# Early weight splits in two batches at wider spacing, operand sets loaded closer together, x stored a step later

## The chip, the core and the metric

The kernel runs on one core of a Trainium2 chip. The core has a matrix engine (TensorE, PE in the profile, with its weight loads as PEld), a vector engine (VectorE, DVE), a scalar engine (ScalarE, ACT), GpSimd (POOL) and a queue engine that here only issues transfers (SyncE, SP). The metric is device time in microseconds of the whole program. Before the change the median of 3 runs is 2904.11 us (2894.93 to 2907.33).

## The reference, cut to what matters

One layer of a decoder step in float32 for 1024 prompt tokens and 64 sample tokens (8 sequences of 8), model width 1024:

```python
x = x + 0.5 * swiglu(rmsnorm(x, norm_ffn1), ffn1_w_in, ffn1_w_out)      # first FFN
mix = token_mixing(rmsnorm(x, norm_mix), ...)                           # projection, pooling and SSD branches
x = x + mix
x = x + 0.5 * swiglu(rmsnorm(x, norm_ffn2), ffn2_w_in, ffn2_w_out)      # second FFN
y = rmsnorm(x, norm_final)

def swiglu(x, w_in, w_out):          # w_in 1024 x 5632, w_out 2816 x 1024
    gu = x @ w_in
    return (silu(gu[..., :2816]) * gu[..., 2816:]) @ w_out
```

`token_mixing` multiplies by `w_in` (1024 x 8224), runs a causal pooling branch (`pool_w_group`, `pool_w_out`) and a chunked SSD scan (`ssd_w_out`), gates them and multiplies by `w_o`. The new pooling, convolution and SSD states are outputs too.

## The kernel before, in words

**Number format.** Each float32 operand of a large product is cut into a high part that TensorE takes at full rate and the remainder: `hi = round(x)` on ScalarE, `lo = x - hi` on VectorE. A product is then three matmuls: weight-high by hi, weight-high by lo, weight-low by hi. Weights come from HBM as 128 x 512 pieces of 256 KB (`wraw`) and are cut into `wh` and `wl`.

**Stages in time.** First FFN: three plain column blocks, then pairs by a seven-product (Strassen-like) scheme, `pw`, which needs seven sums of weights, cut one after the other; its results go through GpSimd into seven operand sets in HBM (`hc...`). The output product (`po`) runs through these seven sets one by one (list `OUTER`, index p): each set is 11 tiles `hr`, loaded back and cut into `hh` and `hr`, while the set before is multiplied; the sums land in x tiles. Projection stage: the same seven-product scheme over `w_in` pairs (`pw` again), with convolution, pooling window sums and gates behind each pair. Then the mixing stage (scan, `pso`, `pwo`), and the second FFN, with the same code as the first.

**Early splits.** The weights that are used more than once later (four column blocks of `w_in`, the pooling group weights, `pool_w_out`, `ssd_w_out`, `w_o` and the plain blocks of the second FFN) are cut ahead of time by `part_weights`: 88 jobs, in the order of the list `early`. In step i the generator issues the load of job i (`wr`, L354), then the two stores of job i-2 (high part L361, low part L362, 256 KB each, to a DRAM tile `wp`), then the split of job i-1 (ScalarE L403, VectorE L405, both in `split`). Later stages load the ready parts (L342). Each job takes two tiles of the stage's shared ring `fx` (16 tiles, tag `fx`), which also holds the results of the pairs, x tiles and temporaries.

**What sets the order.** The program is written as generators ("chains"). `pe[0]` is a planner's clock that counts matmul time in us; a chain yields how long it wants to wait, and `tick()` after each matmul group steps the chains that are due. `later(d, fn)` is a chain of one step. A scheduler then orders the instructions of each engine, gives tiles their buffers, and puts waits where a buffer has to come free. All large transfers go through SP's queue in order: a transfer that waits for its source or for a buffer holds those behind it. The number of transfers under way is bounded as well: the issue of one waits for the end of one some eight issues earlier.

**The numbers that the change touches.** `W_AT, W_NEXT = 108.0, 3.7` start the early splits at planner time 108 and space their steps. `H_AT[1]`, `H_PACE[1]` (3.0 and 2.5) say when, after the start of set p, the loads of set p+1 begin, and their spacing; index 0 is for the first set. In the output product of the first FFN finished x tiles are written to HBM (`xspill`, L819) right after they are merged (L786) and squared for the next norm. The second FFN uses `H_AT` and `H_PACE` as well, but stores no x there.

Of the kernel before, what the change touches and what calls it, by code (L numbers as in the profile page):

```python
# [75 lines left out]
N_PRE = 3  # L76
Y_PACE = 0.8
G_WAIT, G_LAST, GP_LAST = (6.0, 12.0), (2.5, 3.0), (2.5, 1.2)
H_AT, H_PACE, H_LAND, H_CUT = (1.0, 3.0), (0.9, 2.5), 4.5, 0.9
N_SUM = 1  # L80
B_AT, B_PACE, HN_WAIT = 3.0, 7.0, 22.0
W_AT, W_NEXT = 108.0, 3.7
AHEAD = 4
ACC_AT, RD_WAIT, Y_LOAD = 4.0, 6.0, 0.6

# [2 lines left out]
def tile_hybrid_pool_ssd_macaron(  # L88
# [11 lines left out]
    dma = nc.sync.dma_start  # L100
# [7 lines left out]
    def nm(s):  # L108
        uid[0] += 1
        return f"{s}_{uid[0]}"  # L110
# [20 lines left out]
    def fx(dt=F32, name="x"):  # L131
        if stage["name"] == "mix":
            return act((P, 576), dt, name)
        return stage["p"].tile([P, FXW], dt, tag="fx", bufs=N_FX, name=nm(name))

    def psum(tag="ps", name="ps"):
        npd = stage["npd"]
        return stage["ps"].tile([P, 512], F32, tag=tag, bufs=npd if tag == "pd" else 8 - npd, name=nm(name))
# [4 lines left out]
    pe = [0.0]  # L143
# [13 lines left out]
    def start(gen, delay=0.0):  # L157
        c = Chain(gen, delay)
        chains.append(c)
        return c  # L160

    def later(delay, fn):
        def g():
            fn()
            return
            yield

        return start(g(), delay)
# [9 lines left out]
    def tick():  # L178
        while chains:
            c = min(chains, key=lambda q: q.due)  # L180
            if c.due > pe[0]:
                return
            c.step()
# [5 lines left out]
    def mm(out, lhsT, rhs, start=True, stop=True, free=False):  # L189
        pin(T.matmul(out, lhsT, rhs, start=start, stop=stop, skip_group_check=free))  # L190
        pe[0] += max(out.free_size(), 64) / 2400.0 * (1 if rhs.dtype == F32R else 4)
# [90 lines left out]
    xspill = [[dp.tile([P, NTOK[h]], F32, tag=f"xs{h}_{m}", name=f"xspill{h}_{m}") for m in range(KD)] for h in HALVES]  # L282
# [60 lines left out]
            out.append(t.bitcast(F32R).rearrange("p (k c) -> p k c", c=ncol))  # L343
        return out

    def part_weights(jobs):


        held, t0 = {}, pe[0]
        for i in range(len(jobs) + 2):  # L350
            if i < len(jobs):
                w, k0, nk, c0, ncol = jobs[i]
                t = fx(name="wr")[:, : nk * ncol]
                dma(t.rearrange("p (k c) -> p k c", c=ncol),  # L354
                    w[k0 * P : (k0 + nk) * P, c0 : c0 + ncol].rearrange("(k p) c -> p k c", p=P))
                held[i] = t, fx(F32R, name="wp")[:, : nk * ncol]
            if i >= 2:
                w, k0, nk, c0, ncol = jobs[i - 2]
                t, a = held.pop(i - 2)
                d = dp.tile([P, 2, 4 * P], F32, tag=f"wp{len(parted)}", name=nm("wp"))  # L360
                dma(d[:, 0, : nk * ncol], a.bitcast(F32))  # L361
                dma(d[:, 1, : nk * ncol], t)  # L362
                parted[id(w), k0, c0] = d
            if 1 <= i <= len(jobs):
                t, a = held[i - 1]
                split(t, a, t.bitcast(F32R))
            yield max(0.1, t0 + W_NEXT * (i + 1) - pe[0])

    def products(out, Wh, Wl, kk, cs, xs, k, nk):
        for ps_, (W, lo_) in enumerate(((Wh, False), (Wh, True), (Wl, False))):  # L370
# [30 lines left out]
    def split(src, hi, lo, scale=1.0):  # L401

        S.activation(hi, src, AF.Identity, scale=scale)  # L403
        if isinstance(scale, float) and scale == 1.0:
            V.tensor_tensor(lo, src, hi.bitcast(F32), op=ALU.subtract)  # L405
        else:
            V.scalar_tensor_tensor(lo, src, scale, hi.bitcast(F32), op0=ALU.mult, op1=ALU.subtract)
# [297 lines left out]
    def ffn(wi, wo, prep, after, half=None, sums=None):  # L705
# [17 lines left out]
        def feed(p):  # L723


            hi, lo = parts[p] = [], []
            todo, last, k = [], 0.0, 0
            while k < N_K2 or todo:
                if k < N_K2:
                    t, a = act(name="hr")[:, :HALF_T], act((P, 576), F32R, "hh")[:, :HALF_T]  # L730
                    dma(t, hc[OUTER[p][0]][k])
                    todo.append((pe[0], t, a))
                    k += 1
                    yield H_PACE[p > 0]
                while todo and todo[0][0] + H_LAND < pe[0] and last + H_CUT < pe[0] or k == N_K2 and todo:
                    if k == N_K2:
                        yield max(0.2, todo[0][0] + H_LAND - pe[0], last + H_CUT - pe[0])
                    _, t, a = todo.pop(0)
                    split(t, a, t.bitcast(F32R))
                    hi.append(a)  # L740
                    lo.append(t.bitcast(F32R))
                    last = pe[0]

        def out_raw(blocks, m, kb, nk):

            raws = [raw_w(wo, ki * N_K2 + kb, nk, (mi * 4 + m) * P) for mi, ki, _ in blocks]
            if len(raws) == 1:
                return raws[0]
            t = stage["p"].tile([P, 4 * P], F32, tag="wsum", bufs=N_S, name=nm("ws"))[:, : nk * P]
            with tc.high_priority(hp[0]):  # L750
                G.tensor_tensor(t, *raws, op=ALU.add if blocks[1][2] > 0 else ALU.subtract)  # L751
            return t

        def out_weights(t, nk):

            wh, wl = (sp.tile([P, 4 * P], F32R, tag=n_, bufs=N_W, name=nm(n_))[:, : nk * P] for n_ in ("wh", "wl"))
            with tc.high_priority(hp[0]):
                S.activation(wh, t, AF.Copy)
                V.tensor_tensor(wl, t, wh.bitcast(F32), op=ALU.subtract)  # L759
            return [w.rearrange("p (k c) -> p k c", c=P) for w in (wh, wl)]  # L760
# [14 lines left out]
        def x_tile(h, m):  # L775
            if xs[h][m] is None:
                xs[h][m] = t = fx(name="x")[:, : NTOK[h]]
                dma(t, xspill[h][m])
# [9 lines left out]
        for p, (_, blocks, dests) in enumerate(OUTER):  # L788
            if p + 1 < len(OUTER):
                feeds[p + 1] = start(feed(p + 1), H_AT[1])  # L790
            for m in range(4):
                for mi in sorted({d[0] for d in dests}):
                    for h in HALVES:
                        x_tile(h, mi * 4 + m)
                pts = [psum("pd", "po") for _ in range(2)]
                for kb in range(0, N_K2, 4):
                    n4 = min(4, N_K2 - kb)
                    while len(summed) <= min(at + N_SUM, len(chunks) - 1):
                        summed.append(out_raw(*chunks[len(summed)]))
                    wh, wl = out_weights(summed[at], n4)  # L800
                    summed[at] = None
                    at += 1
                    for kk in range(n4):
                        k = kb + kk
                        while len(parts[p][0]) <= k:
                            feeds[p].step()
                        hi, lo = parts[p][0][k], parts[p][1][k]
                        for i, (W_, X_) in enumerate(((wh, hi), (wh, lo), (wl, hi))):
                            for j, pt in enumerate(pts):
                                mm(pt[:, :HT], W_[:, kk, :], X_[:, j * HT : (j + 1) * HT],  # L810
                                   start=k == 0 and i == 0, stop=k == N_K2 - 1 and i == 2)
                        tick()
                for mi, ti, sign in dests:
                    merge(pts, mi, m, ti, sign)
                if p in ENDS and sums:
                    h, q = ENDS[p]
                    x = xs[h][q * 4 + m]
                    squares(sums[h], x)
                    dma(xspill[h][q * 4 + m], x)  # L819
            if p in ENDS:  # L820
                h, q = ENDS[p]
                if half and p in (1, 5):
                    half(h, q, xs[h])
                if p in (4, 6):
                    after(h, xs[h])
# [119 lines left out]
    early = [(W, kb, 4, c0, P) for c0 in [OFF_Z + j * P for j in range(N_ZP)] for kb in (0, 4)]  # L945
# [57 lines left out]

    start(turn(), TURN_AT)
    start(load_consts(), CONST_AT)
    start(part_weights(early), W_AT)
    hp[0] = HP
    ffn(wi1, ffn1_w_out[0], prep1, after1, sums=sums1)

# [193 lines left out]
    def pool_in():  # L1203
        src = state_pool[0].rearrange("b r d -> (b r) d")
        sin = []
        for q in range(2):
            t = fx(name="spin")[:120]
            dma(t[:, :512], src[:, q * 512 : (q + 1) * 512])
            sin.append(t)
        return sin, [fx(name="ost")[:79] for _ in range(2)]  # L1210
# [118 lines left out]
        ends.clear()  # L1329

    zs = list(range(N_ZP, 16, 2))
    sin, ost = pool_in()
    for k in range(0, KD, 2):
        u_pair(k, sin, ost)
# [644 lines left out]
```

## Time and profile before

| what | value |
|---|---|
| runs, median (range) | 2904.11 us (2894.93 to 2907.33) |
| profiled execution, its own time | 2903.95 us |
| its span, first to last instruction | 2902.1 us |
| mean granted TensorE clock | 0.988 |
| PE busy | 2789.8 us, 96% |
| DVE, ACT, POOL busy | 1802.6, 1339.0, 1189.0 us (62%, 46%, 41%) |
| moved by DMA | 595.61 MB, mean 205 GB/s |
| `pw` of the first FFN, first to last matmul | 110.8 to 562.9 us |
| `po` of the first FFN | 563.1 to 818.2 us |
| `pw` of the projection stage | 874.6 to 1524.8 us |
| `pw` and `po` of the second FFN | 2231.1 to 2638.8 and 2638.9 to 2885.3 us |
| early splits, first to last (ACT) | 146.9 to 544.3 us |

In a table of stretches each row has the stretch in us, its length, then for each engine the busy time and in brackets the number of instructions, the granted clock as a share of full speed, the busy share of the DMA engines, and GB/s. A list of waits has "engine, line waited for <- what ended the wait: us in total, times, longest".

### The profile page before, as it was taken

What the parts mean: (1) busy time and instruction counts of PE and PEld (TensorE: products, weight loads), DVE (VectorE), ACT (ScalarE), POOL (GpSimd) and SP (SyncE); (2) the same over time, 40 slices, a digit from 0 to 9 for tenths busy, and PEclk for the clock granted to TensorE, in tenths of its full rate; (3) what the DMA queues carried; (4) which work ended last, traced back from release to release, by engine and by line L of the source; (5) the groups of instructions that cost most, each with busy time, mean ns of one, the idle gap of its engine ahead of it and who ended that gap; (6) DMA issues with size and microseconds to landing.
All of it is one profiled execution on the core that took longest, in us unless ns stands there. A gap on an engine that the chain in (4) does not pass through costs nothing. (4 is left out here: it accounts for less than half of the span.)

```text
span 2902.1 us, 56345 instructions
## 1 busy us (share of the span) xinstructions
PE 2789.8 (96%) x20898; PEld 2660.8 (92%) x20898; DVE 1802.6 (62%) x2949; ACT 1339.0 (46%) x2830; POOL 1189.0 (41%) x1152
## 2 busy tenths in 40 slices
PE   7999999899999999999999989999999999999998
PEld 6998999899989999999997777778999999999997
DVE  6555566766765787566745775765346544448764
ACT  5344444533443456555556765554123333335433
POOL 5444546624243333343421333543115654554422
PEclk9999999999999999999999999999999999999999
DMA  5588899898763333233349879988875422339864
GB/s 138 158 273 268 293 296 290 282 278 263 244 209 111 112 102 119 91 101 110 107 139 314 277 283 307 326 289 251 278 256 184 150 94 94 98 98 298 266 204 158
DMA packets 614725, 595.61 MB, mean 205 GB/s; under 512 B 56922, under 2 KB 430800, under 8 KB 614442
## 3 DMA queue, kind: packets, MB, share of 16 engines
q1 hardware_dynamic: 613078, 589.62, 63.3%
q8 instruction: 164, 2.69, 0.4%
q10 hardware_dynamic: 1372, 2.40, 0.2%
q14 instruction: 111, 0.91, 0.1%
HBM read 419.52 MB, written 172.58 MB: 204 GB/s over the span
## 5 line engine op out<-in xcount | busy, mean ns | idle before, releaser
L190 PE MATMUL pw<-hi,wh 128*128 128x288 f32 (+1 forms) x2176 | 634.4, 292 | 16.1 <-ACT t L604 8.3
L190 PE MATMUL pw<-X,wh 128*128 128x256 f32 (+1 forms) x3264 | 626.2, 290 | 10.5 <-ACT t L602 5.8
L190 PE MATMUL pw<-hi,wl 128*128 128x288 f32 (+1 forms) x2176 | 631.0, 290 | 5.4 <-DVE wl L502 5.4
L190 PE MATMUL pw<-lo,wh 128*128 128x288 f32 (+1 forms) x2176 | 629.6, 289 | 0.0
L190 PEld LDWEIGHTS pw<-X,wh 128*128 128x128 f32 x3264 | 516.5, 190 | 13.8 <-ACT t L602 7.9
L190 PE MATMUL pw<-X,wl 128*128 128x256 f32 (+1 forms) x1632 | 471.2, 289 | 0.8 <-DVE wl L502 0.8
L190 PEld LDWEIGHTS pw<-hi,wh 128*128 128x128 f32 x2176 | 414.2, 190 | 21.0 <-ACT t L604 9.8
L190 PEld LDWEIGHTS pw<-hi,wl 128*128 128x128 f32 x2176 | 413.9, 190 | 7.3 <-DVE wl L502 7.2
L190 PEld LDWEIGHTS pw<-lo,wh 128*128 128x128 f32 x2176 | 414.3, 190 | 0.0
L502 DVE TENSOR_TENSOR wl<-s,wh 128x512 fp32r<-128x512 f32 x284 | 255.9, 903 | 200.9 <-ACT wh L501 195.6
L495 POOL TENSOR_TENSOR s<-wraw,wraw 128x512 f32<-128x512 f32 x142 | 202.8, 1428 | 359.8 <-DVE wl L502 165.4
L190 PEld LDWEIGHTS pw<-X,wl 128*128 128x128 f32 x1632 | 311.0, 191 | 1.1 <-DVE wl L502 1.0
L501 ACT ACTIVATE wh<-s 128x512 fp32r<-128x512 f32 x284 | 179.0, 630 | 234.5 <-PE pw L190 172.2
L751 POOL TENSOR_TENSOR ws<-wraw,wraw 128x512 f32<-128x512 f32 (+1 forms) x120 | 165.4, 1381 | 275.2 <-DMA wraw<-in_ffn_w_out_dram 155.9
L190 PE MATMUL po<-hh,wh 128*128 128x272 f32 x1232 | 259.6, 292 | 9.2 <-ACT hh L403 6.6
L190 PE MATMUL po<-hh,wl 128*128 128x272 f32 x1232 | 258.8, 291 | 4.2 <-DVE wl L759 4.0
L190 PE MATMUL po<-hr,wh 128*128 128x272 f32 x1232 | 257.7, 290 | 1.6 <-DVE hr L405 1.6
L502 DVE TENSOR_TENSOR wl<-wraw,wh 128x512 fp32r<-128x512 f32 x213 | 176.7, 830 | 80.0 <-ACT wh L501 74.0
L190 PEld LDWEIGHTS po<-hh,wh 128*128 128x128 f32 x1232 | 196.8, 190 | 11.3 <-ACT hh L403 7.1
L501 ACT ACTIVATE wh<-wraw 128x512 fp32r<-128x512 f32 x213 | 133.7, 629 | 155.2 <-PE pw L190 137.7
L190 PEld LDWEIGHTS po<-hh,wl 128*128 128x128 f32 x1232 | 196.9, 190 | 6.1 <-DVE wl L759 5.9
L190 PEld LDWEIGHTS po<-hr,wh 128*128 128x128 f32 x1232 | 196.8, 189 | 2.3 <-DVE hr L405 2.3
(397 smaller groups left out, 5538.7 us busy)
## 6 DMA issues: line engine op xcount, KB each, us to landing
wraw<-in_ffn_w_out_dram SPq DMA_DIRECT2D x192, 256.0 KB
wraw<-in_ffn_w_in_dram SPq DMA_DIRECT2D x184, 256.0 KB
wraw<-wp SPq DMA_DIRECT2D x176, 256.0 KB
wraw<-in_w_in_dram SPq DMA_DIRECT2D x124, 256.0 KB
wp<-wp SPq DMA_DIRECT2D x88, 256.0 KB
wp<-wr SPq DMA_DIRECT2D x88, 256.0 KB
wh<-wp SPq DMA_DIRECT2D x88, 256.0 KB
wl<-wp SPq DMA_DIRECT2D x88, 256.0 KB
```

The source lines that it names most:

```text
L190: pin(T.matmul(out, lhsT, rhs, start=start, stop=stop, skip_group_check=free))
L495: G.tensor_tensor(t, a, b, op=op)
L501: S.activation(wh, a, AF.Copy)
L502: V.tensor_tensor(wl, a, wh.bitcast(F32), op=ALU.subtract)
L751: G.tensor_tensor(t, *raws, op=ALU.add if blocks[1][2] > 0 else ALU.subtract)
```

## The change

Three edits. `part_weights` takes its spacing as an argument, and the 88 jobs are started in two batches: the first 36 in the first FFN at planner time 108 with spacing 8.0, the other 52 in the projection stage, from planner time 20 after the start of its pairs, with spacing 9.0. The loads of the operand sets after the first begin at 2.0 instead of 3.0 and are 2.2 instead of 2.5 apart, in both FFNs. The store of a finished x tile in the first FFN is put 2.0 planner us later.

```diff
-H_AT, H_PACE, H_LAND, H_CUT = (1.0, 3.0), (0.9, 2.5), 4.5, 0.9
+H_AT, H_PACE, H_LAND, H_CUT = (1.0, 2.0), (0.9, 2.2), 4.5, 0.9
...
-W_AT, W_NEXT = 108.0, 3.7
+W_AT, W_NEXT, N_EARLY = 108.0, (8.0, 9.0), 36
...
-    def part_weights(jobs):
+    def part_weights(jobs, pace):
...
-            yield max(0.1, t0 + W_NEXT * (i + 1) - pe[0])
+            yield max(0.1, t0 + pace * (i + 1) - pe[0])
...
-                    dma(xspill[h][q * 4 + m], x)
+                    later(2.0, lambda h=h, i=q * 4 + m, x=x: dma(xspill[h][i], x))
...
-    start(part_weights(early), W_AT)
+    start(part_weights(early[:N_EARLY], W_NEXT[0]), W_AT)
...
     zs = list(range(N_ZP, 16, 2))
+    start(part_weights(early[N_EARLY:], W_NEXT[1]), 20.0)
```

How the order of instructions moves is shown at three places. The first is SP's queue in the first FFN, at the store of the mixture `hcs_2_269` (operand set s3, tile 2). Before:

```order
L354 DMA wr_2347<-in_pool_w_group_dram 128x2x256
L361 DMA wp_2350<-wp_2237 128x512
L362 DMA wp_2350<-wr_2235 128x512
L361 DMA wp_2405<-wp_2292 128x512
L362 DMA wp_2405<-wr_2290 128x512
L659 DMA hcb_2_258<-g_2085 128x544
L354 DMA wr_2402<-in_pool_w_group_dram 128x2x256
L361 DMA wp_2486<-wp_2349 128x512
L362 DMA wp_2486<-wr_2347 128x512
L521 DMA wraw_2683<-in_ffn_w_in_dram 128x4x128
L666 DMA hcs_2_269<-s_408_2429 128x544
```

And now:

```order
L354 DMA wr_2343<-in_w_in_dram 128x4x128
L361 DMA wp_2479<-wp_2235 128x512
L362 DMA wp_2479<-wr_2233 128x512
L644 DMA hcs_2_280<-g_2069 128x32
L666 DMA hcs_2_269<-s_393_2389 128x544
L643 DMA hcd_2_247<-g_2023 128x512
L907 DMA xin_400_2456<-in_x_prompt_dram 128x512
L354 DMA wr_2476<-in_w_in_dram 128x4x128
L354 DMA wr_2587<-in_w_in_dram 128x4x128
L361 DMA wp_2590<-wp_2345 128x512
L362 DMA wp_2590<-wr_2343 128x512
```

Ahead of this store there stood two loads and six stores of early splits in eleven rows (eight of eleven); now one load and two stores stand ahead of it, and at that point the jobs are at the blocks of `w_in` and no longer at the pooling weights.

The second is ScalarE's queue in the projection stage, at the start of a pair (`rb` takes the first product `pw`; `ct` is the convolution of the pair before). Before:

```order
L1026 COPY rb_14650<-pw_2499_14636 128x256
L1088 ACTIVATE ct_14653<-ra_14385,cols 128x512
L1088 ACTIVATE ct_14653<-crs_14620,cols 128x64
L501 ACTIVATE wh_14768<-s_2512_14725 128x512
L1026 COPY rb_14672<-pw_2503_14658 128x288
L1097 ACTIVATE ct_14653<-ct_14653 128x576
```

And now:

```order
L1026 COPY rb_14418<-pw_2413_14404 128x256
L1088 ACTIVATE ct_14421<-ra_14137,cols 128x512
L1088 ACTIVATE ct_14421<-crs_14388,cols 128x64
L501 ACTIVATE wh_14544<-s_2429_14501 128x512
L1026 COPY rb_14440<-pw_2417_14426 128x288
L403 ACTIVATE wp_14316<-wr_14314 128x512
L501 ACTIVATE wh_14586<-s_2438_14584 128x512
L1097 ACTIVATE ct_14421<-ct_14421 128x576
```

An early split (L403) now stands between the copy of a product and the next weight split (L501); behind it the queue goes on as before.

The third is SP's queue in the output product of the first FFN, from tile 9 of the operand set b22 (`hcb_9_265`) on. Before:

```order
L731 DMA hr_8201<-hcb_9_265 128x544
L305 DMA wraw_8364<-in_ffn_w_out_dram 128x4x128
L305 DMA wraw_8401<-in_ffn_w_out_dram 128x3x128
L305 DMA wraw_8403<-in_ffn_w_out_dram 128x3x128
L305 DMA wraw_8440<-in_ffn_w_out_dram 128x4x128
L305 DMA wraw_8442<-in_ffn_w_out_dram 128x4x128
L305 DMA wraw_8480<-in_ffn_w_out_dram 128x4x128
L305 DMA wraw_8482<-in_ffn_w_out_dram 128x4x128
L305 DMA wraw_8519<-in_ffn_w_out_dram 128x3x128
L819 DMA xspill_7_91<-x_7671 128x512
L731 DMA hr_8262<-hcb_10_266 128x544
L731 DMA hr_8299<-hcs_0_267 128x544
```

And now:

```order
L731 DMA hr_7773<-hcb_9_265 128x544
L305 DMA wraw_7953<-in_ffn_w_out_dram 128x4x128
L305 DMA wraw_7990<-in_ffn_w_out_dram 128x3x128
L731 DMA hr_7812<-hcb_10_266 128x544
L305 DMA wraw_7992<-in_ffn_w_out_dram 128x3x128
L305 DMA wraw_8029<-in_ffn_w_out_dram 128x4x128
L305 DMA wraw_8031<-in_ffn_w_out_dram 128x4x128
L305 DMA wraw_8064<-in_ffn_w_out_dram 128x4x128
L305 DMA wraw_8066<-in_ffn_w_out_dram 128x4x128
L819 DMA xspill_7_91<-x_7255 128x512
L731 DMA hr_7861<-hcs_0_267 128x544
L731 DMA hr_7902<-hcs_1_268 128x544
```

The last tile of the set, `hcb_10_266`, stood ten rows behind tile 9 and behind the store of x tile 7; now it stands three rows behind tile 9 and ahead of that store.

## The prediction

> **What bounds the kernel now.** I read the stretches first, then the waits of PE, ACT and SP in those that lose time. One stretch serves as the measure: the pairs of the second FFN, the same code as the first FFN's without early splits.
>
> ```profile
> 110.00:142.00 32.00, 32.00 (x257) 32.00 (x256) 16.29 (x29) 14.48 (x34) 18.32 (x17) 1.00 0.54 174
> 142.00:546.00 404.00, 379.21 (x2907) 372.60 (x2906) 243.40 (x373) 181.35 (x407) 212.28 (x186) 0.98 0.87 283
> 546.00:598.00 52.00, 45.89 (x332) 43.87 (x332) 40.61 (x63) 23.90 (x46) 29.64 (x22) 0.97 0.95 302
> 875.00:1430.00 555.00, 553.38 (x4388) 550.35 (x4387) 387.33 (x689) 288.35 (x582) 206.66 (x293) 1.00 0.34 105
> 2249.00:2612.00 363.00, 363.00 (x2884) 363.00 (x2883) 179.57 (x258) 137.90 (x292) 204.55 (x192) 1.00 0.34 107
> 2612.00:2664.00 52.00, 47.03 (x358) 45.28 (x357) 45.24 (x61) 27.03 (x51) 31.23 (x23) 1.00 0.89 279
> ```
>
> TensorE is the bound. In 2249 to 2612 it is never idle and does 2884 matmuls in 363 us, 7.945 a us. At that rate the 2907 of 142 to 546 take 365.9 us; they took 404. So the stretch with the early splits loses 38.1 us. Before they start (110 to 142) nothing is lost, and the projection stage loses little: 4388 matmuls are worth 552.3 of 555 us. Who makes PE wait:
>
> ```profile
> PE pw L190 <- ACT t L604: 8.3, 6, 5.0
> PE pw L190 <- ACT t L602: 5.6, 5, 2.3
> PE pw L190 <- ACT t L594: 3.6, 2, 3.3
> PE pw L190 <- DVE t L606: 3.3, 6, 1.8
> ```
>
> ACT copies products out of PSUM (L594, L602, L604) too late, though it is under half busy (181.35 of 404 us). What held ACT and DVE, in the same stretch:
>
> ```profile
> ACT wp L403 <- DMA wr<-in_ssd_w_out_dram: 18.0, 10, 3.8
> ACT wp L403 <- DMA wp<-wr: 15.3, 8, 3.2
> ACT wp L403 <- DMA wr<-in_w_o_dram: 12.4, 7, 4.7
> ACT wp L403 <- DMA wp<-wp: 12.3, 7, 3.5
> DVE wr L405 <- ACT wp L403: 86.7, 52, 5.7
> DVE g L599 <- DMA wp<-wp: 9.7, 3, 4.5
> SPq L354 <- POOL g L612: 7.8, 3, 5.3
> ```
>
> An early split stands in ACT's order at a fixed place; when its load has not landed, or its ring tile's last store has not ended, everything behind it waits. One such event in order of time, on ACT and then on SP:
>
> ```profile
> 232.96 0.36 ACT L594 COPY t<-pw 128x256 f32<-128x256 f32 x1
> 239.63 0.63 ACT L403 ACTIVATE wp<-wr 128x512 fp32r<-128x512 f32 x1 [6.31 <-DMA wr<-in_pool_w_out_dram]
> 240.16 0.61 ACT L501 ACTIVATE wh<-s 128x512 fp32r<-128x512 f32 x1
> 240.69 0.38 ACT L594 COPY t<-pw 128x288 f32<-128x288 f32 x1
> ```
> ```profile
> 230.75 0.33 SPq L907 DMA_DIRECT2D xin<-in_x_prompt_dram  x1
> 236.50 0.38 SPq L354 DMA_DIRECT2D wr<-in_pool_w_out_dram  x1
> ```
>
> SP sat for 5.3 us on a ring tile that GpSimd had not released, issued the load at 236.50, and ACT stood until 239.63; the copy that PE needed came out at 240.69. The clock then drops for some microseconds more:
>
> ```profile
> 170.00:184.00 14.00, 9.03 (x54) 8.83 (x53) 7.95 (x16) 5.80 (x13) 6.15 (x7) 0.76 0.76 245
> 396.00:408.00 12.00, 10.21 (x69) 9.97 (x68) 9.89 (x13) 4.06 (x8) 6.50 (x6) 0.86 0.83 292
> 640.00:656.00 16.00, 11.78 (x74) 11.30 (x73) 11.20 (x15) 5.13 (x10) 7.25 (x6) 0.79 0.92 280
> 784.00:796.00 12.00, 9.35 (x60) 8.91 (x59) 9.06 (x14) 5.10 (x9) 5.70 (x4) 0.86 1.03 328
> ```
>
> A mean clock of 0.76 over 14 us is 3.4 us lost beside the 5.0 us of waiting; at 396 PE was idle for only 1.8 us and 0.14 x 12 = 1.7 us followed at the lower clock. [...]
>
> **The change, part by part.**
>
> *A. 52 of 88 splits leave the first FFN, the rest go at half the rate.* What a split costs there depends on where it falls:
>
> ```profile
> 161.00:363.00 202.00, 186.40 (x1411) 182.35 (x1409) 112.94 (x187) 87.33 (x203) 101.75 (x90) 0.97 0.84 276
> 363.00:444.00 81.00, 74.95 (x573) 73.63 (x571) 52.49 (x71) 37.31 (x82) 43.77 (x38) 0.98 0.92 296
> 444.00:521.00 77.00, 76.24 (x604) 75.77 (x603) 52.50 (x76) 36.09 (x78) 42.97 (x37) 1.00 0.89 284
> L403 ACT ACTIVATE wp<-wr x88: 612/632/650, 146.9 to 544.3; 128x512 fp32r<-128x512 f32 x88
> L405 DVE TENSOR_TENSOR wr<-wr,wp x88: 676/693/1809, 147.6 to 544.9; 128x512 fp32r<-128x512 f32 x88
> ```
>
> 88 splits in 397.4 us are 0.221 a us. At 7.945 matmuls a us the three stretches lose 24.4, 8.9 and 1.0 us, so 0.55, 0.50 and 0.06 us a split. The remaining 36 would lose 2 us at the lowest price and 20 at the highest. Which end is nearer follows from the DMA share. A job moves 3 x 256 KB = 0.786 MB; 88 are 69.2 of the 114.3 MB (283 GB/s x 404 us), leaving 45.1; 36 jobs bring 28.3 back: 73.4 MB, 182 GB/s, share 0.87 x 182/283 = 0.56. At 0.54 (row 110 to 142) nothing was lost, but no splits ran there, and the ring with its late releases stays. I take 0.22 a split, 8 us. **A = -30 us** (-18 to -36).
>
> *B. The output product.* At 640 to 656, 74 matmuls at 7.9 a us are worth 9.3 of 16 us; at 784 to 796, 60 are worth 7.6 of 12: 6.7 and 4.4 us, together 11. Both are one event:
>
> ```profile
> PE po L190 <- ACT hh L403: 6.6, 2, 4.2
> SPq L819 <- DVE x L786: 19.4, 8, 5.3
> 642.42 0.48 SPq L819 DMA_DIRECT2D xspill<-x  x1
> 642.99 1.45 SPq L731 DMA_DIRECT2D hr<-hcb  x1
> 647.89 0.66 ACT L403 ACTIVATE hh<-hr 128x544 fp32r<-128x544 f32 x1 [7.57 <-DMA hr<-hcb]
> ```
>
> The set's last tile was issued at 642.99, behind the store of x that waits for the merge. Now it stands ahead of that store, and planned 1.0 + 10 x 0.3 = 4.0 us earlier, against a wait of 4.2. I take 9 of 11. The turn from pairs to output (546 to 598) loses 52 - 332/7.945 = 10.2 us; the second FFN's (2612 to 2664) 52 - 358/7.945 = 6.9 with no early splits, so up to 3.3 more; I take 2. The second FFN gets the closer loads too, with no x store to pass: 0. **B = -11 us** (-15 to +4: closer loads at a share of 0.9 could delay weight loads by one wait like the 4.2).
>
> *C. 52 splits in the projection stage.* ACT gets 52 x 0.632 = 32.9 us, DVE 52 x 0.693 = 36.0. On 555 us ACT goes from 0.52 to 0.58, DVE from 0.70 to 0.76. DMA: 40.9 MB over 52 x 9.0 planner us, which last about 10 us each (88 x 3.7 = 326 planner us took 397 with 38 lost, so 1.1): 520 us, 79 GB/s more, share 0.34 x 184/105 = 0.60. Cover is PE itself, as long as copies and weight splits come in time. Bounds: nothing (share 0.57 with 73.00 of 73.00 us in the row below), or the price of the worst stretch, 52 x 0.55 = 29 us. The window sums are the tight place:
>
> ```profile
> 1000.00:1150.00 150.00, 148.38 (x1174) 146.67 (x1174) 114.59 (x221) 83.72 (x167) 53.12 (x75) 1.00 0.34 107
> 2176.00:2249.00 73.00, 73.00 (x505) 70.12 (x504) 45.62 (x65) 26.84 (x64) 42.13 (x39) 1.00 0.57 185
> ```
>
> There DVE is 0.76 busy and PE lost 150 - 1174/7.945 = 2.2 us; 15 splits bring DVE to 0.83. I take **C = +4 us**, near the low end: a split comes only every 10 us, while its load has that long to land. [...]
>
> Sum: -30 - 11 + 4 = **-37 us**. The profiled execution took 2903.95 us with a span of 2902.1; 2903.95 - 37 = 2867. The median of the runs, 2904.11, is the same number. **Forecast 2867 us.**
>
> **The rivals.**
>
> 1. *The waits were the FFN's own.* The ring and late weight sums hold ACT and POOL, and the early splits only fill the gaps. For it: SP's 5.3 us wait was for GpSimd, and full rate cost nearly nothing in 444 to 521. Against it: the same code without early splits loses nothing in 2249 to 2612. Then the 36 cost the highest price and more, A = -12, B = -6, C = +4: 2890.
> 2. *The ring fills in the projection stage.* A job holds two tiles for two steps and its stores, about 2 x (18 + 4)/9 = 5 of 16 tiles, where none were held. If a pair's `ra` or `rb` then waits for a tile, the copy of its first product (L1026) is late and PE stops with the clock behind it: at the wait and drop of 396, 1.8 + 1.7 = 3.5 us. A pair is 7 products x 2 halves x 12 = 168 matmuls, 21 us at 7.945 a us, so the 520 us of splits lie beside 25 pairs. One such stop in every second pair (12 x 3.5 = 42 us) cancels the 41 us of A and B, and with one in each pair, 25 x 3.5 = 88, the kernel takes 2904 - 41 + 88 = 2951. For it: splits blocked ACT just so in the first FFN. Against: the projection stage shows 2.7 us of loss now, DMA at 0.60 returns tiles sooner than at 0.87.
> 3. *The change does more than I take:* all remaining splits at the lowest price (A = -36), B = -15, C = 0: 2853.
>
> **How the numbers follow.** Forecast (with 3 as its good end) 0.77, of which rival 3 has 0.15; rival 1 0.13; rival 2 0.10, of which 0.06 lies well past the point where the gain is gone. The forecast's own range is 2850 to 2885. To leave out no more than 0.2 I reach over rival 1: **2848 to 2893**. Within 0.5% of 2904 is 2889.6 to 2918.6, about what a measurement of this kernel can tell from no change. Faster takes 0.77, most of the other half of rival 1 (0.06) and a part of rival 2 (0.02): 0.85; same 0.09; slower 0.06.
>
> **What would show it.** In the profile after, `pw` of the first FFN should last about 422 instead of 452 us, waits of ACT L403 for `wr` there should nearly vanish, and the DMA share should be near 0.56. In the output product PE's wait for `hh` should be under 2 us and SP's wait at L819 shorter. In 890 to 1430 DMA should be near 0.60 and PE lose under 8 us; a wait of PE for L1026 or L1030 in each pair would be rival 2. The forecast is wrong if the first FFN keeps its stalls at a share below 0.6, or if the projection stage gets longer than the first FFN gets shorter.

## The result, and the profile after

| | before | after |
|---|---|---|
| median of the runs | 2903.03 us (2894.93 to 2907.33, 4 runs) | 2865.39 us (2859.53 to 2875.76, 4 runs) |
| profiled execution, span | 2902.1 us | 2863.5 us |
| mean granted clock | 0.988 | 0.993 |

The changed kernel takes 0.9877 of the time before, 95% interval 0.9841 to 0.9913: 36 us less at the middle, and faster by more than the measurement's 0.5%. The forecast was 2867 us.

By stage, from the first to the last matmul of each in the two traces (us):

| stage | before | after | difference |
|---|---|---|---|
| first FFN, pairs (`pw`) | 452.1 | 416.8 | -35.3 |
| first FFN, output product (`po`) | 255.1 | 242.5 | -12.6 |
| next norm's product (`pz`) | 56.1 | 54.8 | -1.3 |
| projection (`pw`) | 650.3 | 659.0 | +8.7 |
| second FFN, pairs | 407.7 | 407.7 | 0 |
| second FFN, output product | 246.3 | 248.0 | +1.7 |

They sum to -38.8, and the spans differ by 38.6. The stretches of the kernel after, columns as before (us, length, PE, PEld, DVE, ACT, POOL busy with counts, clock, DMA share, GB/s):

```profile
142.00:546.00 404.00, 400.42 (x3154) 398.19 (x3153) 243.78 (x367) 179.64 (x393) 232.71 (x203) 1.00 0.65 210
142.00:500.00 358.00, 357.29 (x2838) 356.38 (x2837) 202.62 (x314) 154.74 (x346) 204.48 (x182) 1.00 0.63 203
506.00:529.00 23.00, 20.14 (x137) 19.08 (x137) 19.77 (x29) 16.59 (x33) 9.93 (x7) 0.93 0.90 280
841.00:1391.00 550.00, 542.27 (x4284) 537.64 (x4283) 425.66 (x733) 303.75 (x620) 210.53 (x287) 1.00 0.56 177
```

In 142 to 546 there are now 3154 matmuls where there were 2907. At 7.945 a us they are worth 397.0 us, so 7.0 us are lost, and the clock is 1.00. But the pairs now end at 528 us, so this stretch holds their last steps, which cost 23 - 137/7.945 = 5.8 us and in which no early split runs: the last of the 36 starts on ACT at 465.9 us. Before the change these steps lay at 541 to 563 and cost 22 - 130/7.945 = 5.6 us:

```profile
541.00:563.00 22.00, 18.27 (x130) 16.72 (x129) 19.94 (x28) 13.90 (x29) 9.53 (x6) 1.00 1.00 323
```

Up to 500 us, where all 36 splits lie, only 358 - 2838/7.945 = 0.8 us are lost.

In the projection stage 4284 matmuls are worth 539.2 of 550 us: 10.8 us lost at a DMA share of 0.56, where before 4350 matmuls in 550 us lost 2.5:

```profile
890.00:1440.00 550.00, 548.38 (x4350) 545.31 (x4349) 387.49 (x693) 288.40 (x580) 201.11 (x287) 1.00 0.34 106
```

What ACT waited for at the early splits, after the change, in 142 to 546 (line waited for <- what ended the wait: us in total, times, longest):

```profile
ACT wp L403 <- DMA wr<-in_ssd_w_out_dram: 7.1, 3, 3.3
ACT wp L403 <- DMA wr<-in_w_in_dram: 6.7, 2, 3.8
ACT wp L403 <- DMA wp<-wr: 4.8, 2, 4.3
ACT wp L403 <- DMA wp<-wp: 4.0, 1, 4.0
ACT wp L403 <- DMA wr<-in_pool_w_out_dram: 1.1, 1, 1.1
```

The waits for loads (`wr`) fell to 14.9 us and those for ring tiles (`wp<-`) to 8.8. Before, with 88 splits in this stage and not 36, the four rows shown with the prediction alone came to 58.0 (30.4 for loads, 27.6 for ring tiles). In the output product (520 to 830 us) PE's waits are:

```profile
PE po L190 <- DVE wl L759: 1.5, 2, 1.2
PE po L190 <- ACT wh L758: 0.8, 1, 0.8
```

The 6.6 us of waiting for `hh` are gone. So is most of a loss at the start of `po`, which in the kernel before was 35 - 226/7.945 = 6.6 us in the first 35 us, and is 0.4 us now. Before and after:

```profile
563.00:598.00 35.00, 30.73 (x226) 29.85 (x225) 23.61 (x41) 12.93 (x24) 20.85 (x16) 0.95 0.92 291
528.00:563.00 35.00, 34.99 (x275) 34.65 (x274) 28.70 (x43) 13.06 (x23) 20.38 (x16) 1.00 0.98 311
```

### The profile page after: what moved, and what is told of

The parts are those of the page before. It is cut to its first block, busy times and chain, and to the rows that moved or that the text cites. A ratio compares the mean times of both kernels' runs of the same rounds, so it can differ in the third digit from the quotient of the medians.

```text
span 2863.5 us, 56390 instructions
## 1 busy us (share of the span) xinstructions
PE 2776.3 (97%) x20898; PEld 2649.0 (93%) x20898; DVE 1812.1 (63%) x2949; ACT 1338.3 (47%) x2830; POOL 1191.9 (42%) x1152
## 5 line engine op out<-in xcount | busy, mean ns | idle before, releaser
L502 DVE TENSOR_TENSOR wl<-s,wh 128x512 fp32r<-128x512 f32 x284 | 266.2, 939 | 198.7 <-ACT wh L501 195.4
L501 ACT ACTIVATE wh<-s 128x512 fp32r<-128x512 f32 x284 | 179.2, 631 | 263.3 <-PE pw L190 207.9
L190 PE MATMUL po<-hr,wh 128*128 128x272 f32 x1232 | 255.7, 288 | 0.1
L502 DVE TENSOR_TENSOR wl<-wraw,wh 128x512 fp32r<-128x512 f32 x213 | 165.9, 779 | 89.0 <-ACT wh L501 82.6
L501 ACT ACTIVATE wh<-wraw 128x512 fp32r<-128x512 f32 x213 | 133.7, 629 | 176.0 <-PE pw L190 157.2
```

The lines of the kernel that those rows point to most:

```text
L501: S.activation(wh, a, AF.Copy)
L502: V.tensor_tensor(wl, a, wh.bitcast(F32), op=ALU.subtract)
```

## The experiments

Each ratio is against runs of the kernel before on the same chip, with its 95% interval; the stage times are from one profiled execution of each. On the other chips the median of before was 2895 to 2902 us.

**Which edit does it: operand sets and store alone.** The early splits stay as before. The edit of the kernel before:

```diff
-H_AT, H_PACE, H_LAND, H_CUT = (1.0, 3.0), (0.9, 2.5), 4.5, 0.9
+H_AT, H_PACE, H_LAND, H_CUT = (1.0, 2.0), (0.9, 2.2), 4.5, 0.9
...
-                    dma(xspill[h][q * 4 + m], x)
+                    later(2.0, lambda h=h, i=q * 4 + m, x=x: dma(xspill[h][i], x))
```

> All 88 early splits stay in the first FFN at spacing 3.7; only the operand sets are loaded closer and x is stored later. My theory (part B works by itself): the output product of the first FFN goes from 255 to about 245 us, the pairs of the first FFN stay at 452 and the projection pairs at 650; the whole takes about 2893 us. Rival (the output product got shorter because the splits had left its start, not by B): it stays at 253 to 255 and the whole at 2902.

Measured: 2896.32 us, ratio 1.0006 [0.9991, 1.0021]. `po` took 250.1 us, about halfway between my theory's 245 and the rival's 253 to 255, and the whole is not faster than before.

**The two batches alone.** Operand sets and store as before. The edit of the changed kernel:

```diff
-H_AT, H_PACE, H_LAND, H_CUT = (1.0, 2.0), (0.9, 2.2), 4.5, 0.9
+H_AT, H_PACE, H_LAND, H_CUT = (1.0, 3.0), (0.9, 2.5), 4.5, 0.9
...
-                    later(2.0, lambda h=h, i=q * 4 + m, x=x: dma(xspill[h][i], x))
+                    dma(xspill[h][q * 4 + m], x)
```

> Only the two batches of splits; operand loads and the x store as before. My theory: pairs of the first FFN 417 us, output product 252 to 253 (only the turn from pairs to output gains), projection pairs 659; the whole 2875. Rival (the output product was helped by the batches): output product 245 or less, the whole 2867 or less.

Measured: 2866.64 us, ratio 0.9890 [0.9873, 0.9907]. Pairs 416.9, `po` 248.5 (my theory had 252 to 253), projection 659.2 us. So nearly the whole gain comes with the batches, and a part of what `po` gained too.

**The batches with the later store, loads as before.**

```diff
-H_AT, H_PACE, H_LAND, H_CUT = (1.0, 2.0), (0.9, 2.2), 4.5, 0.9
+H_AT, H_PACE, H_LAND, H_CUT = (1.0, 3.0), (0.9, 2.5), 4.5, 0.9
```

> The two batches and the later x store, but operand loads at 3.0 and 2.5 as before. If the store ahead of the last operand load was the cause of the two late sets, the output product takes about 244 us as after the change; if the closer loads were, it takes 252 to 253, as with the batches alone.

Measured: 2862.02 us, ratio 0.9880 [0.9865, 0.9895], `po` 245.6 us. In time it can't be told apart from the two batches alone, nor from the changed kernel. But its trace tells the two edits of part B apart: the waits for `hh` are still there (4.3 us, 2 of them), and the last tile of the set is still issued behind the store of x. It is the closer loads that take these waits away, and not the later store.

**Before, profiled again.** Is the pair of stalls in the output product a matter of the order, or of that one execution?

> The kernel before, profiled a second time, for the two stalls of the output product (642 to 648 and 784 to 790 us of its span). If they belong to the order of the loads and the store of x, as term B has it, they recur: the output product of the first FFN takes about 255 us again (254 to 257) and the matmul stream stops there twice for more than 4 us. If they were chance events of that execution, it takes 249 to 252, as it does with the old order of loads in the run with the two batches alone (248.5). The first FFN's pairs should lose their 38 us either way (pw 448 to 456 us), since their stalls come from the order of the splits.

Measured: 2903.97 us, `po` 252.3 us. The stalls recur, at 649 and 789 us. The pairs took 457.9 us, a little over the 448 to 456 that I expected: one execution of the same kernel differs from another by some 6 us there. PE's waits for `hh` in 520 to 830 us of this execution:

```profile
PE po L190 <- ACT hh L403: 5.4, 2, 3.2
```

The same list of the kernel with the two batches alone:

```profile
PE po L190 <- ACT hh L403: 5.5, 2, 4.1
```

Two waits, each time, in all eight kernels or executions whose loads of the sets keep the old order, and none in the six with closer loads. In the kernel with the closer loads alone other waits have grown instead:

```profile
PE po L190 <- DVE wl L759: 4.2, 6, 1.3
PE po L190 <- ACT wh L758: 2.2, 2, 1.8
```

So the mechanism of term B is right, and its price is less than it looked. Over all profiled executions `po` took 254 us on the mean with the old loads and dense splits (251.2 to 255.7, six kernels or executions), 250.1 with closer loads; with fewer splits in the first FFN 247 with the old loads (248.5 and 245.6) and 242.2 with closer ones (240.8 to 244.2, five kernels). By these traces closer loads and the store are worth 4 to 5 us of `po`, and the batches another 7 or 8. Most kernels were traced once, and two executions of the kernel before differ by 2.8 us in `po`; the times of the runs, which allow B alone 2.6 us at best, don't confirm the 4 to 5. The part of the batches lies mainly at the start of `po`: its first 35 us hold 226 matmuls before, 228 with B alone, 264 with the batches alone and 275 after. Early splits don't run into `po` in any of these kernels (the last starts at 544.3 us before, `po` at 563.1). What links their end, now 62 us ahead of `po` and not 19, to its start is not shown.

**Spacing alone.** The changed kernel, but the first batch of 36 at the old spacing.

```diff
-W_AT, W_NEXT, N_EARLY = 108.0, (8.0, 9.0), 36
+W_AT, W_NEXT, N_EARLY = 108.0, (3.7, 9.0), 36
```

> As after the change, but the first 36 splits at spacing 3.7 instead of 8.0. If spacing is what counts (a load needs longer than 3.7 to land), they lose 0.5 us each as before, 18 us, and the pairs of the first FFN take about 432 us. If their number is what counts, they lose 5 us or less and the pairs take 417 to 420 us.

Measured: 2882.35 us, ratio 0.9950 [0.9935, 0.9965]. Pairs 439.0 us, 22 more than after. Stretches of this kernel:

```profile
142.00:320.00 178.00, 161.87 (x1231) 158.99 (x1231) 94.21 (x161) 75.06 (x174) 84.92 (x77) 0.97 0.84 274
320.00:527.00 207.00, 207.00 (x1647) 206.80 (x1647) 106.10 (x158) 81.30 (x177) 115.43 (x106) 1.00 0.37 118
```

While the splits run, 178 - 1231/7.945 = 23.1 us are lost, 0.64 a split; once they are done, nothing. The same 36 splits at spacing 8.0 cost 0.8 us, 0.02 a split.

**The DMA share alone.** In `dense36` the share was also higher while the splits ran (0.84; after the change 0.63 in 142 to 500 us). So the changed kernel was run with extra traffic at its own spacing:

```diff
+            for r in range(4 if pace == W_NEXT[0] else 0):
+                e = dp.tile([P, 4 * P], F32, tag=f"ex{i}_{r}", name=nm("ex"))
+                dma(e, wi2[r * P : (r + 1) * P, :512])
             if i >= 2:
```

> The changed kernel with four more DRAM-to-DRAM copies of 256 KB in each step of the first batch (some 37 MB that nothing reads; splits, ring and spacing as in the changed kernel). It tells the share of the DMA engines from the spacing of the splits. My theory has the two together: a load that shares the engines lands later, so at a share of 0.85 to 0.9 in 142 to 520 us the first FFN's pairs go from 417 to 425 to 440 us and waits of ACT L403 for wr come back (over 20 us in sum). The rival, that the spacing alone counts because a load has 8 us to land, has pw stay at 416 to 421 us with the share up by over 0.2 and the time within 0.3% of the changed kernel's.

Measured: 2891.75 us, ratio 0.9966 [0.9951, 0.9980]. But most of the time over the changed kernel lies ahead of the pairs, which start at 132.6 instead of 111.5 us: 66 of the 152 copies were issued there. The pairs took 427.2 us, 10.4 more than after and within the 425 to 440 of my theory. In the stretch that holds the 36 splits:

```profile
163.00:500.00 337.00, 330.03 (x2587) 327.98 (x2587) 180.59 (x291) 141.27 (x321) 190.35 (x170) 0.99 0.82 267
```

At a share of 0.82 it loses 337 - 2587/7.945 = 11.4 us, and `dense36` 23.1 at 0.84, with as many splits. So transfers that have nothing to do with the splits cost time too, and I can't say that the share is harmless; but at nearly the same share the dense spacing loses twice as much.

**Which wait makes the dense splits dear.** Four kernels relieve one or two waits each of the kernel before, all 88 splits at 3.7. First, a split stands two steps after its load, so that loads have twice the time to land:

```diff
-            if i >= 2:
-                w, k0, nk, c0, ncol = jobs[i - 2]
+            if i >= 3:
+                w, k0, nk, c0, ncol = jobs[i - 3]
...
-            if 1 <= i <= len(jobs):
-                t, a = held[i - 1]
+            if 2 <= i <= len(jobs) + 1:
+                t, a = held[i - 2]
```

> The kernel before (88 splits at a spacing of 3.7 in the first FFN), but each split stands two steps after its load and not one, so a load has about 8 us to land; a ring tile is held one step longer. If ACT's waits for loads that have not landed make the 38 us, most of it goes: pw of the first FFN 425 to 435 us instead of 450, ratio 0.990 to 0.995, with no less DMA traffic. If the stalls come from the ring's late releases or the DMA engines' share, pw stays at 447 to 456 or grows, since more tiles are held: ratio 0.998 to 1.005.

Measured: 2895.87 us, ratio 0.9978 [0.9964, 0.9991], pairs 448.5 us. ACT's waits at the splits in 142 to 520 us:

```profile
ACT wp L403 <- DMA wp<-wp: 26.5, 14, 4.2
ACT wp L403 <- DMA wp<-wr: 21.4, 12, 3.2
...
ACT wp L403 <- DMA wr<-in_w_o_dram: 1.2, 3, 0.5
```

The waits for loads are gone (1.7 us in all), and those for ring tiles have grown from 27.6 to 47.9. Second, with the two steps, the ring tile of the high part is taken only at the split:

```diff
-                held[i] = t, fx(F32R, name="wp")[:, : nk * ncol]
+                held[i] = t
...
-                t, a = held[i - 2]
+                t = held[i - 2]
+                a = fx(F32R, name="wp")[:, : t.shape[1]]
+                held[i - 2] = t, a
```

> The kernel before (88 splits at a spacing of 3.7 in the first FFN) with two edits: a split stands two steps after its load, and the ring tile of its high part is taken only at the split. With two steps alone ACT's waits for loads nearly vanished (1.7 us), but its waits for ring tiles whose stores had not ended grew to 48 us in 142 to 520 us, and pw of the first FFN stayed at 448.5 us. My theory now is that the ring of 16 tiles turns too fast at this spacing: with the tile taken two steps later the waits for ring tiles shrink too, below 20 us, and pw falls to 420 to 435 us, ratio 0.985 to 0.993. The rival, that the wait only changes place again (SP's loads wait for the ring instead, over 40 us, and ACT for the loads), has pw at 440 to 455 us and the ratio at 0.995 to 1.002.

Measured: 2894.40 us, ratio 0.9988 [0.9974, 1.0001], pairs 448.7 us. The waits for ring tiles did not shrink:

```profile
ACT wp L405 <- DMA wp<-wp: 27.2, 13, 3.9
ACT wp L405 <- DMA wp<-wr: 24.8, 14, 4.8
```

Third, the same late tile with the split one step after its load:

```diff
-                held[i] = t, fx(F32R, name="wp")[:, : nk * ncol]
+                held[i] = t
...
-                t, a = held[i - 1]
+                t = held[i - 1]
+                a = fx(F32R, name="wp")[:, : t.shape[1]]
+                held[i - 1] = t, a
```

> The kernel before with one edit: the ring tile of a split's high part is taken at the split and not at the load, one step later; the split still stands one step after its load. By the ring theory it takes away a part of the 28 us in which ACT waits for ring tiles and leaves the 50 us for loads: pw of the first FFN 438 to 448 us, ratio 0.994 to 0.999. If the ring does not matter, pw stays at 450 to 458.

Measured: 2898.90 us, ratio 0.9999 [0.9987, 1.0012], pairs 453.1 us: no effect. Fourth, the stores of the splits go through ACT's queue, so that SP no longer stands until a split is done:

```diff
-                dma(d[:, 0, : nk * ncol], a.bitcast(F32))
-                dma(d[:, 1, : nk * ncol], t)
+                S.dma_start(d[:, 0, : nk * ncol], a.bitcast(F32))
+                S.dma_start(d[:, 1, : nk * ncol], t)
```

> The kernel before (88 splits at a spacing of 3.7 in the first FFN) with one edit: the two stores of each early split are issued by ACT, at the place where SP issued them, a step after the split. The landing time of the loads, the ring and the traffic stay. In the traces so far SP stands at these stores until ACT and DVE have done the split (some 90 us in 142 to 520 us), the FFN's own weight loads are queued behind them, and GpSimd waits 36 to 60 us for those weights in every kernel that stalls and 4 to 7 us in those that do not. If this lockstep of SP with the splits makes the stalls, it goes: GpSimd's wait for weights under 15 us, pw of the first FFN 415 to 430 us, ratio 0.985 to 0.992. If the splits themselves are too dense for the ring and the DMA engines, whoever issues the stores, pw stays at 445 to 458 us, ratio 0.997 to 1.003; ACT's own issuing, some 176 times 0.3 to 0.5 us, could make it longer still.

Measured: 2892.22 us, ratio 0.9972 [0.9958, 0.9985], pairs 444.7 us. GpSimd's wait for the FFN's own weights, in 142 to 520 us of the kernel before:

```profile
POOL s L495 <- DMA wraw<-in_ffn_w_in_dram: 39.3, 9, 12.0
```

And of this one:

```profile
POOL s L495 <- DMA wraw<-in_ffn_w_in_dram: 10.3, 8, 2.9
```

GpSimd's wait fell under 15 us as I had expected, and the pairs, for which I had 415 to 430 us, kept 444.7 all the same. ACT's waits at the splits of this kernel:

```profile
ACT wp L403 <- DMA wr<-in_ssd_w_out_dram: 35.3, 16, 4.1
...
ACT wp L403 <- DMA wr<-in_pool_w_out_dram: 15.3, 7, 3.4
...
ACT wp L403 <- DMA wr<-in_w_o_dram: 14.1, 5, 3.5
```

With the ring and SP relieved, the waits for loads grew. In four kernels ACT's waits at the splits thus moved between loads and ring tiles (`wr` summed over all its sources; ring tiles where a split's own store, `wp<-`, came last). The third row also counts the waits there that something else ended. `dense36` is the changed kernel at 3.7:

| 142 to 520 us | before | two steps | two steps, late tile | late tile | stores by ACT | `dense36` | after |
|---|---|---|---|---|---|---|---|
| waits for loads, us | 49.2 | 1.7 | 2.4 | 56.3 | 79.3 | 18.4 | 14.9 |
| waits for ring tiles, us | 27.6 | 47.9 | 52.0 | 25.2 | 4.7 | 18.9 | 8.8 |
| all waits at the splits, us | 109.9 | 84.1 | 90.4 | 115.1 | 93.6 | 62.3 | 30.6 |
| pairs, us | 452.1 | 448.5 | 448.7 | 453.1 | 444.7 | 439.0 | 416.8 |

The pairs moved by 7.4 us at most, and two executions of the kernel before differ by 6; the whole kernel gained 0.3% at best, where the batches gave 1.1%. So no single one of these waits makes the stall: relieve one and others stand in its place, as long as a job comes every 3.7. With 36 splits ACT waits 1.7 us a split at 3.7 and 0.85 at 8.0, half as much, while TensorE's loss falls from 0.64 us a split to 0.02. Why it falls so much further is not shown. Relieving ring, loads and SP together (two steps, and the stores on ACT's queue) was not tried, so whether they explain the 38 us stays open.

**Where the projection stage's 8.7 us come from.** VectorE has 48.4 us more work there and is 0.77 busy (425.66 of 550 us). Here the low part of the second batch is subtracted on GpSimd:

```diff
-                split(t, a, t.bitcast(F32R))
+                if pace == W_NEXT[1]:
+                    S.activation(a, t, AF.Identity)
+                    G.tensor_tensor(t.bitcast(F32R), t, a.bitcast(F32), op=ALU.subtract)
+                else:
+                    split(t, a, t.bitcast(F32R))
```

> The changed kernel with the low part of the second batch's 52 splits (a - high part) subtracted on GpSimd and not on VectorE. If the 8.7 us that the projection stage got longer come from VectorE's queue (36 us more work at 0.76 busy), they fall to 2 to 5: pw of the projection 652 to 655 us instead of 659, and the kernel 4 to 6 us faster than the changed one (ratio to before 0.985 to 0.987). If they come from ACT's part, or from the ring and the transfers, pw stays at 657 to 660. If GpSimd, slower at it and also between the weight sums, comes late with its own products, pw grows past 662.

Measured: 2881.90 us, ratio 0.9929 [0.9913, 0.9946]. The projection took 677.6 us, 18.6 more than after. Groups of VectorE in 841 to 1391 us (busy us, mean ns | idle before), after the change:

```profile
L502 DVE TENSOR_TENSOR wl<-s,wh 128x512 fp32r<-128x512 f32 x99 | 69.7, 705 | 52.0 <-ACT wh L501 51.9
L502 DVE TENSOR_TENSOR wl<-wraw,wh 128x512 fp32r<-128x512 f32 x74 | 56.7, 767 | 12.7 <-ACT wh L501 11.9
L405 DVE TENSOR_TENSOR wr<-wr,wp 128x512 fp32r<-128x512 f32 x52 | 48.4, 933 | 4.1 <-ACT wp L403 4.0
```

The same groups in this kernel, where the lines stand four further down:

```profile
L506 DVE TENSOR_TENSOR wl<-s,wh 128x512 fp32r<-128x512 f32 x95 | 75.7, 797 | 64.3 <-ACT wh L505 64.0
...
L506 DVE TENSOR_TENSOR wl<-wraw,wh 128x512 fp32r<-128x512 f32 x72 | 62.8, 872 | 14.1 <-ACT wh L505 13.1 <-DMA wraw<-in_w_in_dram 0.4
```

PE's waits for the weights' low part in that stretch, after the change:

```profile
PE pw L190 <- DVE wl L502: 6.7, 9, 1.3
```

And in this kernel, with its stretch as a whole below it:

```profile
PE pw L190 <- DVE wl L506: 11.8, 12, 2.2
```
```profile
841.00:1391.00 550.00, 531.42 (x4148) 525.06 (x4147) 406.34 (x653) 293.86 (x598) 264.96 (x326) 0.99 0.54 171
```

VectorE lost 52 instructions and its remaining ones became slower, 705 to 797 and 767 to 872 ns, while GpSimd ran the subtractions, 51 of them in this stretch, at 1457 ns each. Not all of the 18.6 us comes that way: PE also waited 3.2 us for `dt` (L1260 on VectorE) and 2.5 us for the load of `cin`, which it did not after the change. The run doesn't tell whether VectorE's own queue sets the 8.7 us, because it did not relieve that queue where PE waits for it. It does show that work moved from VectorE to GpSimd comes back in part as slower work on VectorE.

**Another division, as a candidate.** 48 splits in the first FFN at 6.5, 40 in the projection stage at 11.

```diff
-W_AT, W_NEXT, N_EARLY = 108.0, (8.0, 9.0), 36
+W_AT, W_NEXT, N_EARLY = 108.0, (6.5, 11.0), 48
```

> The changed kernel with 48 splits in the first FFN at a spacing of 6.5 and 40 in the projection stage at 11. If a split costs by its spacing (about 0.1 us at 8.0, 0.6 at 3.7), the first FFN's pairs get 2 to 8 us longer than 417 (419 to 425 us) and the projection 2 us shorter (656 to 658): ratio 0.988 to 0.991, not faster than the changed kernel. If the stalls set in only below the time that a load needs to land (about 5 us), the pairs stay at 416 to 419 us and the kernel is 1 to 2 us faster than the changed one (ratio 0.987).

Measured: 2864.23 us, ratio 0.9883 [0.9859, 0.9906]: the same as the changed kernel. Pairs 418.6 us, so 48 splits at 6.5 cost hardly more than 36 at 8.0; projection 659.5:

```profile
841.00:1391.00 550.00, 542.64 (x4273) 537.68 (x4272) 413.98 (x722) 298.43 (x610) 208.72 (x286) 1.00 0.51 160
```

With 40 splits the projection loses 550 - 4273/7.945 = 12.2 us, no less than the 10.8 with 52. So this loss isn't a price per split, as far as one trace of each can tell. The traces show most of the late matmuls at the same places of the stage: 175, 182, 259, 281, 456 and 475 us after its start with 52 splits, 172, 184, 261, 284, 459 and 478 with 40. Before the change PE was late at three of them already, by 0.5 to 1.1 us (174, 181 and 256 us). One, at 1107 us of the kernel after, on VectorE (start, us, line, instructions):

```profile
1101.19 4.15 DVE L1092 SCALAR_TENSOR_TENSOR ct<-rb,cols,ct 128x512 f32<-128x512 f32 x3
1105.27 0.27 DVE L1092 SCALAR_TENSOR_TENSOR ct<-crs,cols,ct 128x64 f32<-128x64 f32 x1
...
1107.64 0.27 DVE L1092 SCALAR_TENSOR_TENSOR ct<-crs,cols,ct 128x64 f32<-128x64 f32 x1
1107.84 0.68 DVE L502 TENSOR_TENSOR wl<-s,wh 128x512 fp32r<-128x512 f32 x1
1108.44 0.68 DVE L405 TENSOR_TENSOR wr<-wr,wp 128x512 fp32r<-128x512 f32 x1
```

A run of convolution steps (L1092) stands ahead of the weight's low part (L502), which PE is waiting for; three of them took 4.15 us. VectorE works without a pause here. That the early splits leave it with less lead when such a run comes is how I read it; no run tests it.

## Why the prediction was right, and where it was not

**The total** (2867 forecast, 2865.39 measured) is right, as is the direction. That it is so near is in part luck: A gave 5 us more than forecast and C took 5 us more, and they offset each other.

**A, the pairs.** -30 was predicted; the pairs got 35.3 us shorter (416.8 us, not 422). That is within the stated -18 to -36, but the price was ten times too high: the 36 remaining splits cost 0.8 us, 0.02 each, where I took 0.22, 8 us. Rival 3 had A right. The step behind the choice failed: "Which end is nearer follows from the DMA share." The share was 0.63 up to 500 us, not 0.56, and yet the loss was below the lowest price (0.06); and at 0.82 to 0.84 roomy splits with extra traffic lost 11.4 us and dense ones 23.1. The spacing of the jobs sets the larger part of the price, and the traffic another.

**The mechanism of A.** That an early split holds up ACT while its load or ring tile is late, and that the copies behind it and then the clock suffer, is what the trace before shows: ACT stood 6.31 us ahead of the split at 239.63 us, TensorE 3.34 us ahead of the matmul at 241.12, and the clock was at 0.50 from 240.62 to 244.03. As a cause it was too narrow: with the waits for loads taken away the pairs kept their length (448.5), with SP's lockstep taken away nearly so (444.7). What the runs show is that splits 3.7 apart stall TensorE whichever of these waits is relieved (pairs of 444.7 to 453.1 us), and splits 6.5 or 8.0 apart hardly do (418.6 and 416.8).

**B, the output product.** -11 was predicted, 9 from the two events and 2 for the turn. `po` got 12.6 us shorter, by other parts. The events went, as the prediction's order of loads has it: PE waits for `hh` not at all instead of 6.6 us. But the step "I take 9 of 11" was too much: in the run of B alone the two places lose 9.5 us less (in the time from each 132nd matmul of `po` to the next, less 132/7.945), and other places of `po` 4.5 us more, among them its end, since smaller waits for the weights (4.2 us at L759 where there were 1.1) come up. That leaves 4 to 5 us by the traces, and in the whole program nothing of it could be measured alone (1.0006 [0.9991, 1.0021], at best 2.6 us). The sign named in the prediction, SP's wait at L819, was 17.2 us after against 19.4: hardly shorter, so it was not what counted. The other 7 or 8 us of the 12.6 belong to the batches, 5 to 6 of them at the start of `po`, where I had put 2 for the turn.

**C, the projection stage.** +4 was predicted, +8.7 measured, inside the bounds of 0 to 29. The DMA share came out at 0.56, near the forecast 0.60, and the loss is 10.8 us in 550, over the 8 that I had set as the limit. Two things were off. A price per split is the wrong form: 40 splits cost as much as 52. And the 36.0 us for VectorE were taken with a median, 693 ns, where a sum needs the mean: L405 has a mean of 933 ns there, so VectorE got 48.4 us. The median there is 685, and the mean in the first FFN before was already 912:

```profile
L405 DVE TENSOR_TENSOR wr<-wr,wp 128x512 fp32r<-128x512 f32 x88 | 80.0, 912 | 97.7 <-ACT wp L403 86.7 <-DMA wr<-in_w_o_dram 4.9 <-DMA wraw<-in_ffn_w_in_dram 3.0
```

So VectorE got 12.4 us more than I had put down. The trace after has them where L405 runs beside a tensor operation of GpSimd: 30 of the 52 do and take 1115 ns on mean, the 22 others 684, and 30 x 0.431 = 12.9 us.

**The rivals.** That the waits were the FFN's own (2890) fell: pairs of 416.8 us. That the ring fills in the projection stage (2951) fell: PE waited for L1026 once, for 0.9 us, and the kernel before has the same wait:

```profile
PE pw L190 <- ACT rb L1026: 0.9, 1, 0.9
```

That the change does more (2853) had A right (-36), the output product too large (-15 against -12.6) and C wrong (0).

## What to carry to other kernels

In this kernel work prefetched into a busy stage cost by how densely its steps stood, more than by how many bytes moved beside them: 36 splits lost 23.1 us at a spacing of 3.7 and a DMA share of 0.84, 11.4 at 8.0 and 0.82, 0.8 at 8.0 and 0.63. At 3.7, mending a single wait only moved the stall. Before crediting a stall with its whole length, look what is late next: two stalls that lost 9.5 us less gave 5. In a sum of durations take the mean and not the median. And before crediting a loss in a stretch to the work you moved, check that the stretch holds the same part of the program in both traces.

## What the runs showed of the hardware that was not expected

**A wait of 1.8 us cost clock and one of 2.3 us did not.** In the kernel before, TensorE stood still for 1.8 us ahead of a matmul at 400.3 us and the clock dropped; it stood still for 2.3 us ahead of one at 371.7 us and the clock stayed at 1.00. The record of the granted clock behind the profile's rows shows in what the two differ. Within each trace all stretches at half clock begin a whole number of times 3.413 us apart, and nearly all last 3.4 or 6.8 us (13 of 14 before, 7 of 8 after). Cut into these windows, the two places look like this:

```profile
366.91:370.33 3.42, 2.52 (x21) 2.32 (x19) 0.59 (x2) 0.52 (x2) 2.33 (x2) 1.00 0.98 334
370.33:373.74 3.41, 2.00 (x15) 2.00 (x16) 2.93 (x5) 2.99 (x8) 2.00 (x3) 1.00 0.71 267
397.63:401.05 3.42, 1.63 (x13) 1.39 (x12) 2.94 (x4) 0.29 (x1) 1.09 (x1) 1.00 0.81 261
401.05:404.46 3.41, 3.41 (x17) 3.41 (x16) 2.40 (x5) 2.13 (x5) 0.76 (x2) 0.50 1.07 398
```

The longer wait is shared by two windows, with 0.9 and 1.4 us idle; the shorter one lies in one, with 1.8 us idle, and the next window runs at half clock. From 120 to 1480 us of the fourteen traces, every window at full clock with more than 1.8 us idle was followed by half clock, and of those with less than 1.6 only one was. Before the change the seven windows with half clock behind them had 1.73 to 3.21 us idle, and the 383 others at full clock at most 1.46; after it the one had 2.14, and the 396 others at most 1.33. In later stages, with other shapes of matmul, drops follow windows with 1.0 to 1.2 us idle too (1.11 in the one at 2121 us before, 1.04 in the one at 2082 after), so idle time alone does not tell them apart. No window had to be idle from end to end: 1.79 of 3.42 us was enough at 397.63.

**The subtractions on VectorE took longer beside a tensor operation of GpSimd: 883 to 1165 ns on mean, and 684 to 691 without one.** With GpSimd 0.48 busy instead of 0.38 (264.96 and 210.53 of 550 us) the weight subtractions on VectorE went from 705 to 797 and from 767 to 872 ns, 13 and 14%, though VectorE had 52 fewer subtractions to do. Sorted by whether a tensor operation of GpSimd ran at the same time, those without one take the same in both kernels: 685 and 690 ns on mean after the change, 686 and 691 with the low parts on GpSimd. Those with one take 883 and 1163, and 1165 and 1157. What changed is how many meet one: 22 of 173, and 50 of 167. L405 itself, after the change, takes 684 ns on mean in 22 cases without and 1115 in 30 with one.
